# The scaling of attention probabilities by the reciprocal of their sums, issued on GpSimd instead of VectorE

## The chip, the core and the metric

The kernel runs on one core of a Trainium2 chip, as one program. The metric is the time of one execution on the device in microseconds (us), here as a median of runs. The core has four engines that compute: TensorE (PE, with its weight loads as PEld), VectorE (DVE), ScalarE (ACT) and GpSimd (POOL). SyncE (SP) issues most of the DMAs. Each engine works through its own list of instructions in order, and waits at an instruction until the semaphores that it names are set.

## What is computed

A layer with a state-space scan, a sparse attention and a mixture of 32 experts is followed by two layers with attention and a convolutional feed-forward part, one of them for two token streams. There are 256 tokens of 1024 features in each stream, in float32. The change concerns the softmax of four attentions. In the reference this is, for the grouped-query attention of the second part:

```python
def attend(q, k, v):
    s = jnp.einsum('bqhgd,bkhd->bhgqk', q, k) * scale
    p = softmax_f32(s).astype(v.dtype)
    return jnp.einsum('bhgqk,bkhd->bqhgd', p, v)

out_x = sweep_query_blocks(lambda qb: attend(qb, k_all, v_all), qx)...
out_c = attend(qc, kc, vc)... if ctx_out else None
```

The four are the selected and window branches of the first block (16 heads, 256 causal keys), the attention of the context stream in layer 0 (16 heads, 256 keys), that of the main stream in layer 0 (16 heads, 512 keys) and the latent attention of the main stream in layer 1 (16 heads, 512 keys).

## The kernel before

**Products of weights.** All weights are float32 and are split for TensorE into a high part and the rest. `split_weight` loads a piece `raw` by SyncE's queue, ScalarE rounds it to `whi` (L198), VectorE subtracts to get `wlo` (L199), and TensorE multiplies three times (L217 to L219). This runs through the whole program and is most of TensorE's and VectorE's work.

**Attention.** `nsa_attend` (first block) and `attend` (the three others) go by steps of two heads and one half or all of the 256 queries. A step has three parts. `scores` multiplies queries by keys into PSUM, takes the maxima on VectorE (L948 or L1465), makes the scaled negative of them (L951 or L1467) and lets ScalarE take the exponential, which also adds up the sums (L955 or L1471). `weigh` takes the reciprocal of the sums on VectorE (L959, L960 or L1477) and multiplies each row of probabilities by it, in place, one instruction for each head and half of queries (L964 or L1480). `turn` transposes the probabilities on TensorE (L973 or L1490) and copies them to SBUF, one head by VectorE and one by ScalarE; `combine` multiplies them by the values (L986 or L1498). The loop issues the scores of step n, `weigh` of step n-1 and `turn` of step n-2, so that the parts of three steps are under way at a time.

In layer 0 the scores are made from split queries and keys, three products for each head (L1710). The first head lies on one half of the array's rows and the second on the other.

**The order.** The attention generators are woven between other work: `weave` takes a unit of the side chains whenever their share of TensorE time is due. What `weave` gives is a sequence of calls only. A scheduler of the framework then orders the instructions of each engine by priorities and by its own estimates of when they can run, so a change of one instruction's engine shifts the order on all of them. Tiles come from rings of buffers by tag: `k2` for probabilities, `lin` and `aux` for PSUM banks.

**GpSimd before.** It does 12 additions of 128x256 beside the first block's attention (L761), powers for the norms (L507, L1551, L1746), and two DMA issues of constants.

Of the kernel before, what the change touches and what calls it, by code (L numbers as in the profile page):

```python
# [13 lines left out]
OP = mybir.AluOpType  # L14
# [65 lines left out]
# The quads of ada columns that are made beside the router and beside layer 0's attention.  # L80
Q2, Q3 = (0,), (1, 2)
# The rings that hold weights loaded ahead for the experts, before and after the phase's buffers are free.
ROOM = ("raw", "k4"), ("raw", "k4", "Q", "raw", "k4")
# How much of a side chain goes beside each step of the main one.
# [4 lines left out]
# The experts by their rank in number of tokens: the order of the units (rank of group, half) and their blocks.  # L89
# [3 lines left out]
# The 8 KB buffers: those of the second part lie where what the first part keeps there is done early.  # L93
# [5 lines left out]
class Kernel:  # L99
# [21 lines left out]
    @contextmanager  # L121
    def banks(self, **bufs):
        """The eight PSUM banks, cut into rings for one part of the program."""
        with self.tc.tile_pool(name="psum", bufs=1, space=bass.MemoryType.PSUM, reuse_waits="tile") as self.psum:
            self.psum_bufs = bufs
            yield

    @contextmanager
    def phase(self, **bufs):
        """Buffers that live for one part of the program."""  # L130
# [6 lines left out]
    def weave(main, *fills):  # L137
        """main with units of each (generator, share) among its own, by their TensorE time. A fill that yields None
        waits for main."""
# [30 lines left out]
    def passing(self, name, tag):  # L170
        """A constant that is needed only once."""
        which, a, n = self.cst_at[name]
        t = self.sb(tag, [P, n], name=name)
        self.A.dma_start(t, self.cst_ap[which][:, a:a + n])
        return t
# [6 lines left out]
    # ---------------------------------------------------------------- weights  # L182
# [5 lines left out]
    def split_weight(self, view):  # L188
        """(hi, lo) of each block of 128 rows of a view [128, n, cols]."""
# [14 lines left out]
    def flush(self):  # L204
        """Evictions are traced after the next weights' split, which TensorE waits for."""
# [15 lines left out]
    def lin_fm(self, W, c0, ncols, act, evict, k0=0, nk=None, more=False):  # L221
        """out^T: features on partitions. W [K, N] in DRAM; act (hi, lo) [128, nk, 256]."""
# [24 lines left out]
    def lin_tm(self, W, c0, ncols, act, evict, chunk=512):  # L247
        """out: tokens on partitions."""
# [25 lines left out]
    # ---------------------------------------------------------------- set-up  # L274
# [73 lines left out]
    def load_fm(self, src, h, tag, eng):  # L348
        """[256, 1024] rows of DRAM -> feature-major h [128, 8, 256]."""
# [16 lines left out]
    # ---------------------------------------------------------------- adaLN  # L366
# [11 lines left out]
    def take_bias(self, stg, dst):  # L378
        """The bias into dst [128, slots, 48], to which the products are added."""
# [5 lines left out]
    def ada_quad(self, W, q, dst, rsel):  # L385
        """Columns 2048q..2048q+2047 of silu(c) @ W onto dst [128, slots, 48]."""
# [17 lines left out]
    def ada_start(self, p):  # L404
        """Shift and scale of the first norm for half of the features, in the order of ada1."""
# [20 lines left out]
    def first_act(self, rb):  # L426
        """The first norm and the first two chunks of the token-major projection, by halves of the features as the
        modulation comes in."""
# [47 lines left out]
    # ---------------------------------------------------------------- norms  # L476
    def square_sums(self, h, nt, st, gain=None):
        """Sums of squares over features (32 times them) into the two columns of st: the column tiles of TensorE add up
        a quarter each."""
# [17 lines left out]
    def rms_bcast(self, h, nt, dim):  # L497
        """1/rms over features, one column per token, on all partitions (PSUM [128, 256])."""
# [11 lines left out]
    def spread(self, r, n):  # L510
        """Columns of r, one value per token, along the free dimension of all partitions."""
# [11 lines left out]
    def modulation(self, gain, ada, slot, vs, vsc):  # L523
        """gain * (1 + scale) and shift, [128, 8] each."""
# [15 lines left out]
    # ---------------------------------------------------------------- first block: projections  # L540
# [26 lines left out]
    def rope(self, x, nh, t, outs):  # L567
        """x [128, nh, 64] token-major, half-split rotation; written to each of outs."""
# [12 lines left out]
    def project_tm(self, act, pss):  # L581
        """dt, q, k/v, gates of the first block, tokens on partitions; the first two chunks are in pss."""
# [8 lines left out]
    def conv_silu(self, dst, ps, wname, bname, m, nm, taps):  # L591
        """Causal depthwise convolution over tokens, then silu."""
# [20 lines left out]
    # ---------------------------------------------------------------- SSD  # L613
# [40 lines left out]
    def ssd(self):  # L654
        """The chunked scan; y (with the skip) replaces the x channels. Yields where TensorE would wait."""
# [90 lines left out]
    def ssd_gate(self, act, sums):  # L746
        """y * silu(z), and its squares summed by group into sums [2][128, 2, 256]."""
# [35 lines left out]
    # ---------------------------------------------------------------- NSA  # L783
# [141 lines left out]
    def nsa_attend(self):  # L925
        """Selected and window branches (causal both: every block is chosen and the window spans the sequence)."""
# [30 lines left out]
        def weigh(i, t):  # L957
# [3 lines left out]
            for a in range(2):  # L961
                for b in range(2):
                    e = probs[i, t, a][:, b, :]
                    V.tensor_scalar(e, e, r[:, a, b:b + 1], None, OP.mult)  # L964
# [41 lines left out]
    # ---------------------------------------------------------------- first block  # L1006
    def sigmoid(self, out, x):
        """By tanh, whose table is the exponential's too."""
# [3 lines left out]
    def tanh_gates(self, act, c0, sg):  # L1012
        """tanh(x / 2): the sigmoid is half of one more."""
# [78 lines left out]
    # ---------------------------------------------------------------- mixture of experts  # L1092
    def router(self, h):
# [35 lines left out]
        def top(x):  # L1129
            """softmax over the 8 columns; its sorted values and their places."""  # L1130
# [847 lines left out]
```

## Time and profile before

| | us |
|---|---|
| median of 3 runs | 1766.12 |
| lowest and highest run | 1764.79, 1771.28 |
| the profiled execution, span from the first to the last instruction | 1765.9 |
| TensorE busy | 1690.6 |
| TensorE weight loads busy | 1379.4 |
| VectorE busy | 1272.3 |
| ScalarE busy | 917.8 |
| GpSimd busy | 42.4 |

The profile gives no other time for its own execution than the span. Busy time is the union of the instructions on an engine. TensorE's instructions overlap, and their ends are modelled, so a busy TensorE is not one at its peak. The granted clock is the share of full speed that TensorE had: 1.0 is 2.4 GHz and 0.5 is 1.2 GHz. A wait is put down to the semaphore that came last.

### The profile page before, as it was taken

Reading aid. Unit: us, or ns where it says so; the run is one execution under the profiler, and the core shown is the slowest. Engines: PE = TensorE matmul, PEld = TensorE weight load, DVE = VectorE, ACT = ScalarE, POOL = GpSimd, SP = SyncE. Lnnn points to the kernel's source line nnn. Section 1 sums busy time; section 2 is a strip of 40 time slices with the busy share of each in tenths; the row PEclk is TensorE's granted clock in tenths of the full one; section 3 lists DMA queues with packets and bytes.
Section 4 is the critical chain, followed back from the end, with each engine's and each line's share of the span. In section 5 each row is a group of like instructions: output and inputs, shape, how many; then the busy total and the mean of one; then the engine's idle time right before and its main releaser. Section 6 shows DMA issues by size and latency. Waiting matters only on the chain. (4 is left out here: it accounts for less than half of the span.)

```text
span 1765.9 us, 36466 instructions
## 1 busy us (share of the span) xinstructions
PE 1690.6 (96%) x12980; PEld 1379.4 (78%) x12980; DVE 1272.3 (72%) x3070; ACT 917.8 (52%) x1901; POOL 42.4 (2%) x48
## 2 busy tenths in 40 slices
PE   7999999999999999999999898999999989999998
PEld 3898777767876578888887554688999866789997
DVE  3997687675667768757756466968777788777876
ACT  2666446863443544534434252656665566556654
POOL 0000000100001000000000001000000000000000
PEclk8999999999999999999999988999999999999999
DMA  9756956849966997998999886234566432246662
GB/s 321 212 150 195 322 175 191 253 133 306 317 201 207 323 318 240 329 328 268 325 347 346 258 299 229 90 122 138 178 183 183 141 120 72 59 141 183 180 186 72
DMA packets 344962, 381.54 MB, mean 216 GB/s; under 512 B 27353, under 2 KB 298454, under 8 KB 344774
## 3 DMA queue, kind: packets, MB, share of 16 engines
q1 hardware_dynamic: 339456, 376.47, 67.2%
q10 hardware_dynamic: 5174, 1.97, 0.4%
q8 instruction: 104, 1.70, 0.4%
q0 software_dynamic: 144, 0.71, 0.1%
q14 instruction: 84, 0.69, 0.1%
HBM read 378.00 MB, written 1.05 MB: 215 GB/s over the span
## 5 line engine op out<-in xcount | busy, mean ns | idle before, releaser
L198 ACT CAST whi<-raw 128x512 fp32r<-128x512 f32 (+2 forms) x752 | 453.9, 610 | 383.9 <-PE lin L219 219.5
L199 DVE TENSOR_TENSOR wlo<-raw,whi 128x512 fp32r<-128x512 f32 (+2 forms) x752 | 502.4, 678 | 161.5 <-ACT whi L198 148.6
L217 PE MATMUL lin<-XA,whi 128*128 128x256 f32 x768 | 220.1, 287 | 1.7 <-ACT XA L465 1.7
L219 PE MATMUL lin<-XA,whi 128*128 128x256 f32 x768 | 219.0, 286 | 0.0
L218 PE MATMUL lin<-XA,wlo 128*128 128x256 f32 x768 | 218.9, 285 | 0.0
L217 PE MATMUL lin<-A,whi 128*128 128x256 f32 x576 | 168.4, 292 | 2.7 <-DVE k L598 1.9
L218 PE MATMUL lin<-A,wlo 128*128 128x256 f32 x576 | 163.5, 284 | 0.0
L217 PEld LDWEIGHTS lin<-XA,whi 128*128 128x128 f32 x768 | 149.3, 194 | 2.6 <-ACT XA L465 2.5
L218 PEld LDWEIGHTS lin<-XA,wlo 128*128 128x128 f32 x768 | 149.2, 194 | 0.7 <-issue 0.4
L219 PEld LDWEIGHTS lin<-XA,whi 128*128 128x128 f32 x768 | 148.9, 194 | 0.3
L217 PEld LDWEIGHTS lin<-A,whi 128*128 128x128 f32 x576 | 109.9, 191 | 33.8 <-issue 14.1
L219 PE MATMUL lin<-A,whi 128*128 128x256 f32 x448 | 127.7, 285 | 0.0
L217 PE MATMUL lin<-CA,whi 128*128 128x256 f32 x416 | 122.0, 293 | 0.3 <-ACT whi L198 0.2
L218 PE MATMUL lin<-CA,wlo 128*128 128x256 f32 x416 | 118.2, 284 | 1.1 <-DVE wlo L199 1.1
L219 PE MATMUL lin<-CA,whi 128*128 128x256 f32 x416 | 117.9, 283 | 0.0
L218 PEld LDWEIGHTS lin<-A,wlo 128*128 128x128 f32 x576 | 110.1, 191 | 0.9 <-issue 0.7
L1621 ACT ACTIVATE cv<-lin,vecs 128x256 f32<-128x256 f32 x132 | 73.9, 560 | 63.0 <-PE lin L219 52.7
L219 PE MATMUL lin<-XB,whi 128*128 128x256 f32 x352 | 99.4, 286 | 0.1
L1622 DVE SCALAR_TENSOR_TENSOR cv<-lin,vecs,cv 128x255 f32<-128x255 f32 x132 | 63.3, 480 | 49.4 <-ACT cv L1621 49.1
L217 PE MATMUL lin<-XB,whi 128*128 128x256 f32 x352 | 98.7, 283 | 0.0
L218 PE MATMUL lin<-XB,wlo 128*128 128x256 f32 x352 | 98.4, 283 | 0.0
L217 PEld LDWEIGHTS lin<-CA,whi 128*128 128x128 f32 x416 | 79.2, 190 | 15.5 <-issue 6.5
(534 smaller groups left out, 3835.0 us busy)
## 6 DMA issues: line engine op xcount, KB each, us to landing
raw<-in_ffn_w_up_dram SPq DMA_DIRECT2D x264, 256.0 KB
raw<-in_ada_w_dram SPq DMA_DIRECT2D x192, 256.0 KB
raw<-in_ffn_w_down_dram SPq DMA_DIRECT2D x132, 256.0 KB
raw<-in_w_in_dram SPq DMA_DIRECT2D x112, 256.0 KB
wx<-in_w_exp_gate_dram SPq DMA_DIRECT2D x112, 256.0 KB
wx<-in_w_exp_up_dram SPq DMA_DIRECT2D x112, 256.0 KB
wx<-in_w_exp_down_dram SPq DMA_DIRECT2D x112, 256.0 KB
raw<-in_w_ada_dram SPq DMA_DIRECT2D x96, 256.0 KB
```

Of the source, the lines that this page charges most:

```text
L198: self.A.copy(hi, raw)
L199: self.V.tensor_tensor(lo, raw, hi.bitcast(F32), OP.subtract)
L217: mm(out, whi, ahi, start=first, stop=False, skip_group_check=True)
L218: mm(out, wlo, ahi, start=False, stop=False, skip_group_check=True)
L219: mm(out, whi, alo, start=False, stop=last, skip_group_check=True)
L1621: A.activation(acc, ps, AF.Identity, bias=self.v(f"fb{i}", m), scale=self.v(f"fw{i}1", m))
L1622: V.scalar_tensor_tensor(acc[:, 1:], ps[:, 0:TOK - 1], self.v(f"fw{i}0", m), acc[:, 1:], OP.mult, OP.add)
```

## The change

In `weigh`, in both functions, the multiplication is issued on `self.G` (GpSimd) instead of `V` (VectorE). Operands, shapes and counts are the same: 64 instructions in `nsa_attend` (32 of 128x128 and 32 of 128x256) and 96 in `attend` (32 of 128x256 and 64 of 128x512). The other lines of the difference are comments.

```diff
@@ nsa_attend, weigh @@
             for a in range(2):
                 for b in range(2):
                     e = probs[i, t, a][:, b, :]
-                    V.tensor_scalar(e, e, r[:, a, b:b + 1], None, OP.mult)
+                    self.G.tensor_scalar(e, e, r[:, a, b:b + 1], None, OP.mult)
@@ attend, weigh @@
             V.reciprocal(sm, sm)
             for a in range(2):
                 for t in range(nt):
-                    V.tensor_scalar(pr[a][:, t, :], pr[a][:, t, :], sm[:, a, t:t + 1], None, OP.mult)
+                    self.G.tensor_scalar(pr[a][:, t, :], pr[a][:, t, :], sm[:, a, t:t + 1], None, OP.mult)
```

The scheduler's new order differs in many places, mostly in the four attentions. Three are shown, as a difference (- before, + after). The first is on GpSimd at the start of layer 0's attention; `s_14950` and `s_15121` are the powers for the norms of two pieces of the queries, `prob` the probabilities of the first steps by number.

```order
 L1551 TENSOR_TENSOR s_14950<-s_14949,mhalf_63 128x8 x2
+L1480 TENSOR_SCALAR prob_15107<-prob_15107,s_15102 128x512
+L1480 TENSOR_SCALAR prob_15108<-prob_15108,s_15102 128x512
 L1551 TENSOR_TENSOR s_15121<-s_15120,mhalf_63 128x8 x2
+L1480 TENSOR_SCALAR prob_15146<-prob_15146,s_15141 128x512
+L1480 TENSOR_SCALAR prob_15147<-prob_15147,s_15141 128x512
```

The powers stand behind the first step's two products, and the next step's products behind the powers.

The second is on TensorE in the middle of layer 0's attention. `lin_15495` and `lin_15496` are the two heads' scores of one step, each made by three products (L1710); `prob_15362` and `prob_15363` are the probabilities that are transposed.

```order
-L1710 MATMUL lin_15495<-khi_14578,qTx_14569 128x512
-L1710 MATMUL lin_15495<-khi_14578,qTx_14570 128x512
-L1710 MATMUL lin_15495<-klo_14571,qTx_14569 128x512
 L1490 MATMUL aux_15460<-ident_58,prob_15362 128x128 x4
 L1490 MATMUL aux_15466<-ident_58,prob_15363 128x128 x4
+L1710 MATMUL lin_15495<-khi_14578,qTx_14569 128x512
 L1710 MATMUL lin_15496<-khi_14578,qTx_14569 128x512
+L1710 MATMUL lin_15495<-khi_14578,qTx_14570 128x512
 L1710 MATMUL lin_15496<-khi_14578,qTx_14570 128x512
-L1710 MATMUL lin_15496<-klo_14571,qTx_14569 128x512
+L1710 MATMUL lin_15495<-klo_14571,qTx_14569 128x512
 L1498 MATMUL acc_15484<-pT_15425,vc_6566 64x256
```

The first head's scores move behind the transposes and stand between the second head's; the second head's last product moves behind the products with the values (L1498).

The third is on TensorE near the end of the first block's attention: the transposes (L973) of the last step but one, and the projection (`lin_4897`) that follows.

```order
 L973 MATMUL aux_4865<-ident_58,prob_4782 128x128 x2
 L973 MATMUL aux_4869<-ident_58,prob_4782 128x128 x2
+L219 MATMUL lin_4897<-D1_3056,whi_4900 128x256
+L217 MATMUL lin_4897<-D0_3055,whi_4906 128x256
 L218 MATMUL lin_4897<-D0_3055,wlo_4907 128x256
 L219 MATMUL lin_4897<-D1_3056,whi_4906 128x256
```

Products of the projection that stood ahead of these transposes stand behind them, so the transposes come earlier in the list.

## Rows read from the trace of the kernel before

**Rows 1.** Head of the page: the span, and each engine's busy us, share, instructions.

```profile
span 1765.9 us, 36466 instructions
...
PE 1690.6 (96%) x12980; PEld 1379.4 (78%) x12980; DVE 1272.3 (72%) x3070; ACT 917.8 (52%) x1901; POOL 42.4 (2%) x48
```

**Rows 2.** Busy time by stretch, us (columns: stretch, length, engines, granted clock, DMA share, GB/s).

```profile
240.00:385.00 145.00, 143.48 (x1038) 102.35 (x1037) 108.87 (x362) 98.49 (x247) 10.32 (x13) 1.00 0.59 185
575.00:630.00 55.00, 52.97 (x435) 28.96 (x436) 39.39 (x111) 28.49 (x88) 0.00 (x0) 1.00 0.96 307
1080.00:1105.00 25.00, 21.43 (x95) 7.38 (x96) 17.18 (x45) 6.71 (x14) 3.23 (x2) 0.80 0.67 224
1105.00:1152.00 47.00, 46.59 (x316) 29.77 (x313) 43.67 (x113) 32.45 (x84) 0.00 (x0) 1.00 0.23 75
1440.00:1530.00 90.00, 87.43 (x483) 58.96 (x482) 73.43 (x207) 56.53 (x133) 0.00 (x0) 1.00 0.19 61
```

**Rows 3.** Waits, 240 to 385 us, then 575 to 630 (waiter <- awaited: us, times, longest).

```profile
PE aux L973 <- DVE prob L964: 0.9, 1, 0.9
...
ACT prob L1471 <- DVE s L1467: 11.6, 5, 5.6
```

**Rows 4.** VectorE's groups by shape (count, busy us, mean ns, idle before).

```profile
L199 DVE TENSOR_TENSOR wlo<-raw,whi 128x512 fp32r<-128x512 f32 x684 | 464.9, 689 | 150.7 <-ACT whi L198 138.6 <-DMA wx<-in_w_exp_up_dram 1.9 <-PE lin L218 1.8
...
L1480 DVE TENSOR_SCALAR prob<-prob,s 128x512 f32<-128x512 f32 x64 | 28.5, 479 | 0.3
...
L1480 DVE TENSOR_SCALAR prob<-prob,s 128x256 f32<-128x256 f32 x32 | 9.8, 346 | 0.1
...
L964 DVE TENSOR_SCALAR prob<-prob,s 128x128 f32<-128x128 f32 x32 | 7.4, 280 | 0.1
```

**Rows 5.** GpSimd's groups by shape: its addition in the first block.

```profile
L761 POOL TENSOR_TENSOR sums<-sums,k 128x256 f32<-128x256 f32 x12 | 9.9, 824 | 332.8 <-ACT k L760 332.8
```

**Rows 6.** Timeline of GpSimd at 282 us; of all engines at 303 (start us, length us).

```profile
282.51 0.94 POOL L761 TENSOR_TENSOR sums<-sums,k 128x256 f32<-128x256 f32 x1 [262.46 <-ACT k L760]
...
303.05 0.73 POOL L761 TENSOR_TENSOR sums<-sums,k 128x256 f32<-128x256 f32 x1 [2.27 <-ACT k L760]
...
303.31 1.01 DVE L199 TENSOR_TENSOR wlo<-raw,whi 128x512 fp32r<-128x512 f32 x1
```

**Rows 7.** Timeline of TensorE in layer 0's attention.

```profile
1111.56 0.73 PE L1710 MATMUL lin<-khi,qTx 64*128 64x512 f32 x4
...
1112.48 0.72 PE L1710 MATMUL lin<-khi,qTx 64*128 64x512 f32 x2
...
1113.37 1.09 PE L1490 MATMUL aux<-ident,prob 128*128 128x128 f32 x8
...
1117.16 1.09 PE L1490 MATMUL aux<-ident,prob 128*128 128x128 f32 x8
1118.18 0.50 PE L1710 MATMUL lin<-khi,qTx 64*128 64x512 f32 x2
```

**Rows 8.** Timeline of VectorE in the same stretch.

```profile
1114.06 0.15 DVE L1477 RECIPROCAL s<-s 128x2 f32<-128x2 f32 x1
...
1114.78 0.87 DVE L1480 TENSOR_SCALAR prob<-prob,s 128x512 f32<-128x512 f32 x2
```

**Rows 9.** Timeline of all engines at the first block's last steps.

```profile
371.94 0.15 DVE L960 TENSOR_TENSOR s<-s,gate 128x4 f32<-128x4 f32 x1
...
373.25 0.63 PE L973 MATMUL aux<-ident,prob 128*128 128x128 f32 x4 [0.88 <-DVE prob L964]
...
378.45 0.16 DVE L960 TENSOR_TENSOR s<-s,gate 128x4 f32<-128x4 f32 x1
...
379.58 1.09 PE L973 MATMUL aux<-ident,prob 128*128 128x128 f32 x8
```

**Rows 10.** Timeline of all engines at layer 1's second step.

```profile
1456.15 0.15 DVE L1477 RECIPROCAL s<-s 128x2 f32<-128x2 f32 x1
...
1457.72 0.71 PE L1490 MATMUL aux<-ident,prob 128*128 128x128 f32 x5
```

## The prediction

> **What bounds the kernel now.** I read the head of the page first. The span is 1765.9 us and TensorE is busy for 1690.6 us of it, 96%; VectorE 1272.3 us, GpSimd 42.4 us [rows 1]. The reader is to see that VectorE, which the change relieves, has over 490 us of spare time, and that TensorE has 75. Then the busy time by stretch, for the four stretches in which attention runs: the first block's (240 to 385 us), the context's beside the experts (575 to 630), layer 0's (1105 to 1152) and layer 1's (1440 to 1530) [rows 2]. TensorE is idle there for 1.52, 2.03, 0.41 and 2.57 us, 6.5 us together. That is all a faster VectorE could give back inside them, unless TensorE's own order gets better. In the second stretch the DMA engines are 96% busy as well, with the experts' weights, so idle time there need not come back at all.
>
> Third, the waits of TensorE. In the first stretch one wait of 0.9 us is for a product of the probabilities [rows 3], and it is the only one that the view puts down to them there. So the multiplication hardly ever ends a wait of the engine that sets the end.
>
> **What goes.** VectorE loses 160 instructions. The 128x512 form takes 479 ns (64 of them), the 128x256 form 346 ns in the later attention (32), the 128x128 form 280 ns (32) [rows 4]; the first block's 32 of 128x256 I take at the same 346. That is 30.7 + 11.1 + 11.1 + 9.0 = 62 us of VectorE's busy time, beside TensorE's work nearly all of it. What I give it on TensorE's path: the 0.9 us wait and a part of the idle time that VectorE's queue causes elsewhere, 1.5 us of the 6.5.
>
> **What comes.** GpSimd gets the same 160 products, and no trace row shows one there. Bounds of a 128x512 product: from below VectorE's own 0.479 us [rows 4]. From above the nearest row on GpSimd, an addition of two 128x256 tensors at 0.824 us on average and 0.73 us where nothing is in its way [rows 5, 6]; twice the size makes 1.46 us, and it reads two tensors where the product reads one and a scalar. I take the middle, 1.0 us, and 0.55 us for 128x256 (between 0.346 and 0.73), 0.4 us for 128x128. The Trainium skill (GPSIMD Engine Reference, section 3.1, Elementwise) gives 769 ns as measured for a tight loop over 512 elements; no run here shows it, and by that price the terms for late products below would shrink to about 0.5 us.
>
> What matters is not GpSimd's sum (about 64 + 35 + 13 = 112 us, in four stretches of 337 us) but how late each product is. In layer 0, VectorE's reciprocal starts at 1114.06, its two products start only at 1114.78, because a copy and a small product stand in front, and TensorE turns the result at 1117.16 [rows 7, 8]. So 2.95 us lie between the end of the reciprocal (1114.21) and the transposes, and GpSimd, which has nothing in front, ends its two by 1114.21 + 0.05 + 2.0 = 1116.3. Two products of 1.0 us per step also fit into a step of 3.3 us (two steps run from 1111.56 to 1118.18, where the 1117.16 transposes take their 1.02 us). I made the same subtraction for the other steps. In layer 0 and layer 1, 28 of the 32 steps have 1.8 us or more to the first transpose. The step at 1456.15 has 1.42 us (end of reciprocal 1456.30, transposes 1457.72) [rows 10], which is enough for the first product and 0.2 us short for the second. The step just ahead of 1105 is some 0.4 us short. In the first block the first ten steps have 14 us and more. Its last ones are tight: products are asked for at 372.09 and wanted at 373.25, asked for at 378.61 and wanted at 379.58 [rows 9]. There two products of 0.55 us come 0.1 to 0.2 us late, the second pair 0.3 us and 0.85 us. I take 1.3 us for the first block, 0.4 for layer 0, 0.2 for layer 1, nothing for the context (its tightest step has 2.35 us for two products of 0.55).
>
> **What the new order does.** The scheduler places everything anew. In layer 0 the six score products of a step are two chains on different halves of the array: interleaved they take 0.92 us (1111.56 to 1112.48), one chain alone takes 0.89 us (1112.48 to 1113.37), so two of them 1.78 [rows 7]. Before, every second step is split in two; after, three of these steps are interleaved up to the last product, which saves 1.78 - 1.2 = 0.6 us each (two interleaved pairs and two single products: 0.34 + 0.23 + 2 x 0.32), and an earlier one too, but two steps near the end become split, for 0.7 us each. Sum: -1.8 - 0.8 + 1.4 = -1.2 us. GpSimd's powers for the norms of the queries (L1551) now stand behind two products in its queue; the products end by about 1086.1 and the power started at 1086.26, so this costs nothing, and up to 1 us if a product takes 1.46.
>
> **What the two engines do to each other.** The trace shows it. While GpSimd's addition ran from 303.05 for 0.73 us, VectorE's subtraction from two SBUF tensors (L199) that started at 303.31 took 1.01 us instead of the group's 0.69 [rows 4] and ended 0.54 us after it. The other way round, an addition started at 282.51 under a VectorE operation took 0.94 [rows 6]. So each product can hold a VectorE operation of that kind for 0.3 us and be held by one as long. 160 products at 0.3 us are 48 us on VectorE at the worst, less than the 62 us it is spared, and TensorE meets only what exceeds its slack. None of TensorE's waits in these stretches is for L199's output, so little of it reaches the path: I take 1.0 us, with 0 and 10 us (a fifth of the 48) as bounds.
>
> **Sum.** 1765.9 - 1.5 + 1.3 + 0.4 + 0.2 - 1.2 + 1.0 = 1766.1 us. The median of the runs, 1766.12, is 0.2 us above the profiled span, which I let stand. I predict 1766 us, with 1761 to 1772 as this case's own range.
>
> **Rivals.**
> 1. GpSimd becomes the late engine (slower). If a 128x512 product takes the upper bound, 1.46 us, and is held 0.3 us by VectorE, two of them make 3.5 us, more than layer 0's step of 3.3: 14 steps x 0.2 = 3 us there. The tight steps then lose about 7 us (1.5 us before 1105, 0.7 at layer 0's end, 2.5 in layer 1, 2.6 in the first block), and a few us of VectorE's delays reach TensorE: 1766 + 3 + 7 + 3 = 1779 us. It decides from 1.65 us per product with its waits on. For it: the collision rows, and that GpSimd's addition is slow for its size. Against: the product has one tensor input, and most steps have 2 us of slack. The Trainium skill (SBUF — State Buffer, Who interferes with whom) has the shared port pair held for a whole instruction by whichever engine starts first; the 303.31 row agrees. Four products in a row in the first block would by that rule hold VectorE longest.
> 2. VectorE's queue is the hidden bound (faster). In the context stretch ScalarE waited 11.6 us for the small product on VectorE that stands in front of the exponential [rows 3], and in layer 0 VectorE is 43.67 us busy of 47 [rows 2]. If all 6.5 us of idle time goes, the new order brings its 1.2, and the 3.6 us in which TensorE is idle from 1080 to 1105 [rows 2] go too: 1765.9 - 11.3 = 1754.6 us. Against: TensorE is busy for 46.59 of layer 0's 47 us, and the wait at 1080 is in front of the first exponential, where no product is late.
> 3. The new order alone moves the time, by when TensorE idles. From 1080 to 1105 the granted clock averaged 0.80 [rows 2], so the half level, 1.2 GHz, stood there for about 0.4 of 25 us, 10 us, after TensorE had sat idle. One such stretch more or less is 5 us at full speed: 1761 or 1771 us.
>
> **Chances.** The forecast 0.56, the first rival 0.19, the second 0.15, the third 0.10. A measurement of this kernel can tell about 0.5%, 8.8 us, from no change. The forecast and the third rival lie within it; of the first rival nearly all is beyond it, of the second most, with a little of the others past either end. That makes faster 0.15, same 0.65, slower 0.20. The range takes in the second rival's near half and the first rival up to its price: 1756 to 1779.
>
> **What would show it.** Right: GpSimd's line on the page at 110 to 160 us and VectorE's near 1215 to 1240; the 128x512 product on GpSimd between 0.8 and 1.2 us; TensorE's idle time in the four stretches within 4 us of the 6.5; two steps of layer 0 in 6.0 to 6.7 us. L199's mean grows by some tens of ns in the first block. Wrong: TensorE waiting for L964 or L1480 on GpSimd step after step, a layer 0 step longer than 3.4 us, or the clock falling in a stretch where it is 1.00 now.

## The result: 13.6 us slower

The changed kernel takes 1780.47 us (median of 4 runs, 1780.28 to 1785.73) where the kernel before takes 1766.86 (4 runs beside it, 1764.79 to 1771.28). The ratio is 1.0077, with a 95% interval of 1.0057 to 1.0097. The forecast was 1766 us with a range up to 1779, so the time lies just past the upper end, and past the 0.5% that was to separate slower from no change. It is the outcome of the first rival, GpSimd as the late engine, and at nearly its price of 1779 us.

The profiled execution spans 1778.6 us (1780.37 with what lies around it), 12.7 us more than that of before. Head of the page of the changed kernel (answers [rows 1]):

```profile
span 1778.6 us, 36677 instructions
...
PE 1690.5 (95%) x12980; PEld 1377.4 (77%) x12980; DVE 1235.5 (69%) x2910; ACT 918.4 (52%) x1901; POOL 226.9 (13%) x208
```

TensorE is busy as long as before in the sum over the whole span, so the 12.7 us show as idle time there; by stretch its busy time moves too, as the rows below show. VectorE lost 37 us where I had summed 62: the durations that I summed overlap (together they fill 55.4 us before), and some of VectorE's other instructions grew. GpSimd gained 184 where I had summed 112, and its groups by shape (count, busy us, mean ns, idle before and what ended it) say why; the last row answers [rows 5]:

```profile
L1480 POOL TENSOR_SCALAR prob<-prob,s 128x512 f32<-128x512 f32 x64 | 100.4, 1586 | 79.8 <-DVE s L1477 56.0 <-PE aux L1490 17.1 <-PE lin L1848 4.2
L964 POOL TENSOR_SCALAR prob<-prob,s 128x256 f32<-128x256 f32 x32 | 33.3, 1058 | 31.7 <-DVE s L960 27.0 <-PE lin L218 3.1 <-ACT prob L955 1.6
L1480 POOL TENSOR_SCALAR prob<-prob,s 128x256 f32<-128x256 f32 x32 | 29.7, 946 | 26.8 <-DVE s L1477 21.9 <-DVE hots L1263 3.4 <-PE S L1687 1.6
L964 POOL TENSOR_SCALAR prob<-prob,s 128x128 f32<-128x128 f32 x32 | 22.5, 718 | 252.9 <-DVE s L960 241.0 <-ACT whi L198 11.9
...
L761 POOL TENSOR_TENSOR sums<-sums,k 128x256 f32<-128x256 f32 x12 | 9.0, 748 | 13.7 <-ACT k L760 13.6
```

Undisturbed, a product takes 1.56, 0.92 and 0.60 us for 512, 256 and 128 columns (medians 1563, 923 and 603 ns). I had taken 1.0, 0.55 and 0.4, with 1.46 and 0.73 as upper ends for the first two. Both are above their upper end, and the third is half as dear again as I took it: the product, which reads one tensor, is slower on GpSimd than the addition of two tensors of the same size in the last row.

Busy time by stretch after (columns as in [rows 2]: PE, PEld, DVE, ACT, POOL, granted clock, DMA share, GB/s):

```profile
240.00:385.00 145.00, 139.69 (x1006) 99.76 (x1004) 94.85 (x299) 97.66 (x246) 65.18 (x77) 1.00 0.57 179
575.00:630.00 55.00, 53.03 (x427) 29.38 (x425) 30.47 (x72) 26.50 (x80) 27.90 (x30) 1.00 0.85 268
1105.00:1152.00 47.00, 42.46 (x265) 23.87 (x264) 34.47 (x77) 26.70 (x66) 34.00 (x22) 1.00 0.41 137
...
349.30:417.00 67.70, 61.64 (x406) 0.97 0.50 160
...
1109.20:1172.00 62.80, 57.49 (x402) 1.00 0.25 83
```

Compared with [rows 2], TensorE's idle time grew from 1.5 to 5.3 us in the first stretch and from 0.4 to 4.5 in layer 0. The last two rows (TensorE's busy time only) are cut at the same TensorE instructions as these two of the kernel before, the end of the first block and layer 0:

```profile
350.00:410.00 60.00, 57.55 (x402) 1.00 0.52 167
...
1100.80:1160.00 59.20, 58.23 (x401) 1.00 0.28 92
```

The first block's end takes 67.7 us instead of 60, layer 0's attention 62.8 instead of 59.2. Of the first block's 7.7 us, 4.1 are longer busy time of TensorE; layer 0's 3.6 are all idle time. What TensorE waits for there, after (355 to 400 us, then 1095 to 1170):

```profile
PE aux L973 <- POOL prob L964: 3.9, 8, 0.6
...
PE aux L1490 <- POOL prob L1480: 4.7, 5, 1.5
```

And the steps themselves. The timelines of the engines, after, in the first block's step that answers [rows 9]:

```profile
372.47 0.16 DVE L960 TENSOR_TENSOR s<-s,gate 128x4 f32<-128x4 f32 x1
...
372.82 5.94 POOL L964 TENSOR_SCALAR prob<-prob,s 128x256 f32<-128x256 f32 x8 [1.59 <-ACT prob L955]
...
373.80 0.44 PE L973 MATMUL aux<-ident,prob 128*128 128x128 f32 x2 [0.64 <-POOL prob L964]
374.70 0.44 PE L973 MATMUL aux<-ident,prob 128*128 128x128 f32 x2 [0.46 <-POOL prob L964]
...
376.50 0.44 PE L973 MATMUL aux<-ident,prob 128*128 128x128 f32 x2 [0.46 <-POOL prob L964]
```

TensorE transposes two 128x128 pieces as each product ends, then mostly waits 0.46 us for the next: its transposes come at GpSimd's beat of 0.90 us. The eight products (two steps, merged by the view) are one unbroken row of 5.94 us. The same in layer 0, from the step that the prediction has just ahead of 1105 (its transposes, at 1114.25 here, started at 1105.79 before):

```profile
1112.62 9.27 POOL L1480 TENSOR_SCALAR prob<-prob,s 128x512 f32<-128x512 f32 x6 [14.08 <-DVE s L1477]
...
1113.87 0.15 DVE L1477 RECIPROCAL s<-s 128x2 f32<-128x2 f32 x1
1114.25 0.66 PE L1490 MATMUL aux<-ident,prob 128*128 128x128 f32 x4 [1.45 <-POOL prob L1480]
1115.79 0.65 PE L1490 MATMUL aux<-ident,prob 128*128 128x128 f32 x4 [0.46 <-POOL prob L1480]
```

Three steps' products stand back to back. The reciprocal that ends at 1114.02 finds GpSimd busy until 1115.73 with the step before.

The next step is that of [rows 7, 8]:

```profile
1123.94 0.15 DVE L1477 RECIPROCAL s<-s 128x2 f32<-128x2 f32 x1
...
1124.28 6.18 POOL L1480 TENSOR_SCALAR prob<-prob,s 128x512 f32<-128x512 f32 x4 [2.38 <-ACT pT L1492]
...
1124.39 0.39 PE L1710 MATMUL lin<-klo,qTx 64*128 64x512 f32 x1
1125.90 0.44 PE L1490 MATMUL aux<-ident,prob 128*128 128x128 f32 x2 [1.12 <-POOL prob L1480]
```

GpSimd is free and starts 0.19 us behind the end of the reciprocal, and the product still comes 1.12 us late. TensorE is done with its scores at 1124.78, only 0.69 us behind the reciprocal. Before, the transposes of this step came 2.95 us behind it: the scheduler's new order leaves less work of TensorE in between.

### The profile page after: what moved, and what is told of

It is laid out like the page before. It is cut to its first block, busy times and chain, and to the rows that moved or that the text cites. A ratio compares the mean times of both kernels' runs of the same rounds, so it can differ in the third digit from the quotient of the medians.

```text
span 1778.6 us, 36677 instructions
## 1 busy us (share of the span) xinstructions
PE 1690.5 (95%) x12980; PEld 1377.4 (77%) x12980; DVE 1235.5 (69%) x2910; ACT 918.4 (52%) x1901; POOL 226.9 (13%) x208
## 5 line engine op out<-in xcount | busy, mean ns | idle before, releaser
L199 DVE TENSOR_TENSOR wlo<-raw,whi 128x512 fp32r<-128x512 f32 (+2 forms) x752 | 504.1, 680 | 175.9 <-ACT whi L198 163.0
L1480 POOL TENSOR_SCALAR prob<-prob,s 128x512 f32<-128x512 f32 (+1 forms) x96 | 130.1, 1372 | 106.6 <-DVE s L1477 77.9
```

What stands on the lines that cost most here:

```text
L199: self.V.tensor_tensor(lo, raw, hi.bitcast(F32), OP.subtract)
L1480: self.G.tensor_scalar(pr[a][:, t, :], pr[a][:, t, :], sm[:, a, t:t + 1], None, OP.mult)
```

## The experiments

Three theories: **A**, the product is dear on GpSimd and comes late; **B**, the two engines hold each other up at SBUF, where their tiles lie; **C**, the scheduler's new order and the clock, not the products. All ratios are to the kernel before, run beside each, with 95% intervals; in us of 1767:

| run | ratio | interval | us |
|---|---|---|---|
| whole change | 1.0077 | 1.0057 to 1.0097 | +13.6 |
| e1 first block only | 1.0041 | 1.0025 to 1.0057 | +7.2 |
| e2 later three only | 1.0045 | 1.0030 to 1.0061 | +8.0 |
| e3 shadow products | 0.9994 | 0.9982 to 1.0006 | -1.1 |
| e5 later three, half products | 1.0009 | 0.9998 to 1.0020 | +1.6 |
| e6 second head only | 1.0033 | 1.0021 to 1.0045 | +5.8 |
| e7 first ten steps only | 0.9999 | 0.9988 to 1.0010 | -0.2 |
| e8 context only | 1.0017 | 1.0007 to 1.0026 | +3.0 |
| e10 two-tensor form | 1.0032 | 1.0018 to 1.0045 | +5.7 |
| e11 layers 0 and 1 only | 1.0028 | 1.0016 to 1.0040 | +4.9 |
| e12 only where there is room | 1.0005 | 0.9991 to 1.0019 | +0.9 |

e4's time answers no theory (below), and e9 was run once (1766.99 us), for its trace.

Where it arises, from one trace each: the n-th TensorE instruction of a line and operand is set against the n-th in the kernel before, and the median difference of their starts is taken at ten cuts (us in the time of before). An entry is what a stage adds to the lag.

| run | to 230 | to 345 | first block's end, to 410 | to 545 | context, to 645 | experts, to 960 | to 1090 | layer 0, to 1160 | to 1435 | layer 1, to 1545 | rest |
|---|---|---|---|---|---|---|---|---|---|---|---|
| whole | 0.6 | -1.3 | 7.7 | 0.0 | 2.2 | 1.8 | -2.6 | 3.6 | -0.7 | 1.6 | -0.3 |
| e1 | -0.4 | -1.4 | 8.3 | 0.3 | 0.2 | 1.2 | -1.5 | -0.1 | -1.3 | 1.3 | -1.1 |
| e2 | -0.2 | 0.0 | 0.7 | 0.1 | 3.1 | 1.0 | -2.2 | 3.4 | 0.2 | 1.7 | -1.1 |
| e3 | 1.3 | 0.1 | 0.1 | 0.4 | 0.9 | 2.4 | -0.6 | 0.1 | -0.4 | 0.1 | 0.0 |
| e5 | 1.2 | 0.0 | 0.4 | 0.1 | 2.2 | 1.5 | -1.0 | -0.5 | 0.2 | 0.0 | -0.2 |
| e6 | 1.0 | 1.0 | 1.4 | 0.2 | 2.0 | 0.4 | -1.8 | -0.6 | 0.3 | -0.8 | 0.0 |
| e7 | 2.0 | -1.2 | 0.2 | 0.1 | 0.0 | 1.6 | -4.2 | 0.2 | -0.4 | 0.4 | -0.1 |
| e8 | 1.3 | -0.1 | 0.0 | 0.1 | 2.4 | 2.5 | -0.7 | 1.2 | 0.3 | 1.0 | -1.2 |
| e10 | 2.1 | -1.0 | 3.3 | 0.4 | 2.0 | 1.8 | -4.4 | -0.3 | -2.2 | 1.2 | -0.2 |
| e11 | -0.3 | 0.0 | 0.0 | 0.0 | 0.0 | 0.2 | -2.6 | 3.0 | -0.4 | 1.7 | -0.4 |
| e12 | 0.7 | -1.0 | 0.7 | 0.1 | 1.6 | 0.5 | 0.1 | 0.3 | -0.1 | 1.6 | 0.1 |

Columns without attention (start, experts, ahead of layer 0) move by 2 us and more whatever the edit, so that is the grain of a single trace. The first block's end and layer 0 stand far above it. The cut at 1090 lies where the granted clock changes (0.50 from 1082.8 to 1093.1 before), and shifts up to 1.5 us between its two neighbours (e10, e12). Cut at TensorE's instructions from the transposes at 1101.33 to the end of layer 0 instead, that stretch takes 58.9 us before, 62.3 to 62.6 in the three runs with whole products there (whole, e2, e11) and 58.0 to 59.6 in all the others.

**e1, first block only, and e2, later three only.** The one line of L1480, or of L964, goes back to VectorE:

```
-  self.G.tensor_scalar(pr[a][:, t, :], pr[a][:, t, :], sm[:, a, t:t + 1], None, OP.mult)
+  V.tensor_scalar(pr[a][:, t, :], pr[a][:, t, :], sm[:, a, t:t + 1], None, OP.mult)
```

> Only the first block's 64 products (L964) are issued on GpSimd; the later three attentions keep theirs on VectorE. In the trace of the changed kernel TensorE's work of the first block's last steps (356 to 408 us) ends some 7.7 us later against the kernel before, and the rest of the loss lies in the later attentions. Theory A (late products: a product costs GpSimd 0.92 us for 128x256 and 0.60 for 128x128, three times what VectorE needs, and TensorE waits for it where a step has less room): 7 us slower than before, 5 to 9, with TensorE waiting for L964's output 3 to 5 us between 355 and 400. Theory B (the two engines hold each other up at SBUF): about as much, so that this run alone doesn't tell A from B. Theory C (the scheduler's new order of the instructions and the clock stretches that come with it, not the products): the first block's order hardly differs, so within 2 us of before.

> Only the later three attentions' 96 products (L1480) are issued on GpSimd; the first block keeps its on VectorE. Theory A: what the first block cost is gone and what the later stretches cost stays, 6 us slower than before, 3 to 8 (context stretch 2, experts 2, layer 0 4, layer 1 1.5, less 2 to 3 that the clock gave back ahead of layer 0); with the run of the first block alone it adds up to the whole change's 13 us. Theory C: all of the 13 us here, since here the order of TensorE's instructions differs most.

Measured +7.2 and +8.0 us, 15.2 together against 13.6, so the parts add up. C expected all of it in e2 and none in e1: C alone falls.

**e3, shadow.** VectorE keeps its products in all four attentions, and on the same line of the first block GpSimd does one more, on a scratch tile:

```
+  self.G.tensor_scalar(shadow[:, 0:P * (t + 1)], shadow[:, 0:P * (t + 1)], r[:, a, b:b + 1], None, OP.mult)
```

> VectorE keeps all its products as in the kernel before. In the first block GpSimd does as many further products of the same sizes, from the same reciprocals at the same time, on a scratch tile that nobody reads, so that only the two engines' effect on each other is left. Theory A: nobody waits for these, so within 2 us of before (1765 to 1769). Theory B (collisions): most of the first block's loss comes without the late products, 5 to 8 us slower than before, and VectorE's two-input operations in 240 to 400 us lengthened by over 10 us in all.

Measured -1.1 us, interval through zero, and 0.1 us at the first block's end. The shadows ran, and both engines felt them (e3's groups from 240 to 400 us, GpSimd then VectorE):

```profile
L964 POOL TENSOR_SCALAR shadow<-shadow,s 128x256 f32<-128x256 f32 x32 | 34.4, 1076 | 28.3 <-DVE s L960 25.4 <-ACT prob L955 0.6
...
L964 DVE TENSOR_SCALAR prob<-prob,s 128x256 f32<-128x256 f32 x32 | 12.7, 454 | 0.1
```

VectorE's product took 454 ns on average; before it was 364 in the same stretch. Collisions are real: the VectorE operations that ran beside GpSimd's took 6.8 us more in all than by the medians of before. None of it reached TensorE. B falls for the first block. For layer 0 no shadow was run, but two traces answer it. GpSimd's products are not held there (1563 ns on average from 1109 to 1172 us, as undisturbed). VectorE's small product in front of the exponential (L1467) is, as its rows for layer 0's attention show, before, after and in e10 (below):

```profile
L1467 DVE TENSOR_SCALAR s<-s 128x2 f32<-128x2 f32 x14 | 2.2, 157 | 0.0
L1467 DVE TENSOR_SCALAR s<-s 128x2 f32<-128x2 f32 x14 | 4.5, 322 | 0.0
L1467 DVE TENSOR_SCALAR s<-s 128x2 f32<-128x2 f32 x14 | 5.0, 360 | 0.0
```

In e10 it is held longest, and e10 loses nothing in layer 0. So B isn't layer 0's loss either.

**e4, half products everywhere.** `pr[a][:, t, 0:n // 2]` and likewise in the first block.

> The changed kernel, with each product done only for the first half of its columns on GpSimd (the other half of the probabilities stays unscaled). TensorE's order is that of the changed kernel but for two places. A product should then take 0.95, 0.60 and 0.45 us for the three sizes, close to what the prediction took for whole ones (1.0, 0.55, 0.4). Theory A: the late products all but go, within 3 us of before (1764 to 1770), and TensorE's wait for L964 and L1480 falls to under 3 us in all. Theory B: half of the loss stays, 6 us slower than before. Theory C: the order is as in the changed kernel, so the whole loss stays, 11 to 14 us slower than before.

Measured 1913.66 us (ratio 1.0834), which answers no theory. With the first block's result changed, the tokens choose other experts and the rest of the program works longer. I should have seen that the router stands behind this attention. Only its trace up to the experts can be read: the first block's end lags 4.5 us, not 7.7, with products of 0.60 and 0.44 us. That is less, but more than A left for the whole kernel (3).

**e5, half products in the later three.** As e2, with `0:n // 2`.

> As the run of the later three attentions, but each of their products is done only for the first half of its columns on GpSimd (the other half stays unscaled; the first block is whole, on VectorE). The order on VectorE, ScalarE and SP's queue is exactly that of the later three, TensorE's but for a few rows; only the price of a product falls, to about 0.95 us for the 128x512 and 0.6 us for the 128x256 probabilities. Theory A (late products): layer 0's 3.5 us and layer 1's loss go, TensorE waits less than 1 us for L1480 from 1080 to 1165 (3.2 us with whole products). Theory C (order): nothing goes, 7.5 us slower than before. I hold A for layers 0 and 1, and C for the context's stretch, where TensorE waits for no product and the weights' loads stand in another order in SP's queue: there 2 to 3 us of lag stay, so 3 to 4 us slower than before in all.

Measured +1.6 us instead of e2's 8.0, with the same order of instructions on nearly all engines. In layer 0 the 3.4 us are gone, and of TensorE's wait, 3.2 us in e2, this is left (1090 to 1165 us):

```profile
PE aux L1490 <- POOL prob L1480: 1.0, 2, 0.5
```

So layer 0's loss hangs on the product's duration. The context's 2.2 us stay, as expected, but I had put the total at 3 to 4.

**e6, second head only.** `(self.G if a else V).tensor_scalar(...)` in both places.

> In all attentions VectorE multiplies the first head of each pair, which TensorE turns first, and GpSimd the second, which it turns half a microsecond later. Theory A: a product of 1.56 us that starts right behind the reciprocal ends inside the second head's room in nearly every step (least 1.46 us in the first block, where two of 0.92 us are wanted, and 1.66 us in layer 0), so nearly all of the late products' loss goes: first block +1 us instead of +8, layers 0 and 1 +1 instead of +4. With 2 to 3 us in the context's stretch for the order of SP's loads: 1 to 4 us slower than before, and 9 us faster than the changed kernel. Theory C: as much order is changed as in the changed kernel, 10 us slower than before or more.

Measured +5.8 us where 1 to 4 was expected. Its trace shows what A expected in the first block (1.4 instead of 7.7) and layer 0 (-0.6), but that execution was the fastest of its six (1770.72). The interval runs from 3.7 to 8.0 us, and the medians differ by 4.2, so the miss may be a small one. What the other executions lose on top is not in the trace and stays open.

**e7, first ten steps only.** `(self.G if i < 5 else V)` in the first block, the rest on VectorE.

> Only the first block's first ten steps (40 of its 64 products, which have 14 us and more to the transposes) are issued on GpSimd; its last six steps, whose room is 1.0 to 5 us, and the later attentions stay on VectorE. Theory A: nothing is late, so the 8 us of the first block's end (356 to 410 us) are gone, no half-clock stretch stands at 384, and the 1.4 us stay that the stretch around 250 us gave back: 1.5 us faster to 1 us slower than before. A rival (GpSimd's products cost the first block something wherever they stand, since VectorE's wider order changes): 3 us slower than before or more.

Measured -0.2 us. Forty products of e1's 64 cost nothing; the 24 of the last six steps cost the 7 us. The length of the first block's end in e7, cut as above:

```profile
350.85:411.03 60.18, 57.49 (x401) 1.00 0.52 164
```

**e8, context only, and e11, layers 0 and 1 only.** `(self.G if nkt == 2 else V)`, and `nkt == 4`.

> Only the context attention's 32 products (beside the experts) are issued on GpSimd. SP's queue is then exactly as in the run of the later three: FFN weights stand ahead of experts' weights. If the context's loss comes from that order: TensorE's work lags 2 to 3 us behind the kernel before at 600 to 650 us, waits for wx from DMA, and some of it is given back ahead of layer 0, so 1 to 4 us slower in all, layers 0 and 1 with no further loss. If it comes from late products in the context (GpSimd's 0.92 us each, four a step): the same lag here, but none in the run with half products. If neither: within 1 us of before.

> Only layer 0's and layer 1's products (64 of 128x512) are issued on GpSimd; SP's queue is as in the kernel before. If the context's loss is its own and the parts add up: no lag at 600 to 650 us, 3 to 4 us of lag from 1090 to 1160, about 1 in layer 1, 4.6 us slower than before in all (3 to 6), which with the context's 3.0 makes the 7.6 us of the later three.

Measured +3.0 and +4.9, 7.9 together against e2's 8.0. In e11 the context's stretch is as before (0.0) and layer 0 lags 3.0. In the context the six traces with its products on GpSimd, whole or half or dealt between the engines, lag 2.0 to 3.1 us, and no matmul of TensorE waits for one of them. What it waits for in e8 and not before (570 to 600 us) is one copy on VectorE and one load of weights:

```profile
PE aux L1490 <- DVE pT L1492: 0.9, 1, 0.9
PE acc L1317 <- DMA wx<-in_w_exp_gate_dram: 0.8, 1, 0.8
```

These are not the price: e11 waits 0.6 us for such a load too and doesn't lag. The scheduler had split pairs of score products that ran interleaved before, and these products (L1687) show the loss themselves (565 to 660 us; before, e8, e11):

```profile
L1687 PE MATMUL S<-kT,qTc 64*128 64x256 f32 x64 | 13.7, 412 | 1.2 <-ACT prob L1471 0.7 <-ACT qTc L1591 0.4
L1687 PE MATMUL S<-kT,qTc 64*128 64x256 f32 x64 | 15.7, 415 | 0.6 <-ACT qTc L1591 0.4
L1687 PE MATMUL S<-kT,qTc 64*128 64x256 f32 x64 | 13.7, 412 | 0.5 <-ACT qTc L1591 0.4
```

The same 64 products keep TensorE busy for 15.6 to 15.7 us in all six, and for 13.7 before and in the runs that leave the context alone (e1, e3, e7, e11). That price of the order is C's share: TensorE's own work, not a wait. The queue of loads isn't it: by the names of the tensors SP issues in e2, e5 and e8 in the order of before until some 690 us, and the lag has come by 627. e12, whose context products are those of before, lags 1.6 us there for another reason: its granted clock was 0.50 from 582.36 to 585.77, and the lag comes in that one step.

**e9, the price by itself.** On a scratch tile in the first block, four forms in turn (written out here, in the edit one function):

```
+  G.tensor_scalar(o, o, k, None, OP.mult)      G.tensor_scalar(o, o, 0.5, None, OP.mult)
+  G.tensor_tensor(o, o, k.to_broadcast([P, o.shape[1]]), OP.mult)      G.tensor_copy(o, cmp_rep)
```

> The price by itself. VectorE does all products as before; in the first block GpSimd does 64 operations on a scratch tile that nobody reads, in four forms in turn (heads pairs 0 and 4, 1 and 5, 2 and 6, 3 and 7): product by a scalar per partition, product by a constant, product with the reciprocal spread as a second tensor, plain copy; on 128x128 and 128x256. If a product with a scalar per partition is what is dear: 0.60 and 0.92 us for it, 0.45 and 0.73 us for the two-tensor form (the addition's size), and the constant and the copy at or under these. If GpSimd is as slow with any form: all four within 0.1 us of 0.60 and 0.92.

GpSimd's groups in e9 (means, with VectorE's interference):

```profile
L928 POOL TENSOR_SCALAR shadow<-shadow,s 128x256 f32<-128x256 f32 x8 | 9.4, 1173 | 11.5 <-DVE s L960 10.9
L928 POOL TENSOR_SCALAR shadow<-shadow 128x256 f32<-128x256 f32 x8 | 7.9, 989 | 0.6
...
L928 POOL TENSOR_TENSOR shadow<-shadow,s 128x256 f32<-128x256 f32 x8 | 5.2, 652 | 2.0 <-DVE s L960 1.5
L928 POOL COPY shadow<-cst 128x256 f32<-128x256 f32 x8 | 4.8, 599 | 0.4
```

The shortest of each are 922, 847, 612 and 400 ns. A tensor by a scalar is the dearest form; that the scalar is one per partition adds only 75 ns. The constant was not cheap, against what I expected. The product of two tensors, one of them the reciprocal spread along the row, does the same arithmetic in two thirds of the time.

**e10, the two-tensor form in the real kernel.** The change with

```
+  self.G.tensor_tensor(pr[a][:, t, :], pr[a][:, t, :], sm[:, a, t:t + 1].to_broadcast([P, n]), OP.mult)
```

and the same in the first block; every engine's order is that of the changed kernel.

> The changed kernel with each product written as a product of two tensors (the reciprocal spread along the row) instead of a tensor and a scalar per partition; the order of the instructions is the same on every engine. If that form costs what GpSimd's addition costs (0.73 us for 128x256, about 1.2 to 1.4 us for 128x512), theory A makes the loss fall between that with half products and that with whole ones: 6 to 10 us slower than before instead of 13.6. If the form costs the same or more: 13 us or more. Theory C: 13 us whatever the form costs.

GpSimd's groups in e10:

```profile
L1480 POOL TENSOR_TENSOR prob<-prob,s 128x512 f32<-128x512 f32 x64 | 66.7, 1064 | 106.8 <-DVE s L1477 71.9 <-PE aux L1490 22.4 <-PE lin L1848 5.8
L964 POOL TENSOR_TENSOR prob<-prob,s 128x256 f32<-128x256 f32 x32 | 22.8, 743 | 35.7 <-DVE s L960 33.9 <-ACT prob L955 1.8
L1480 POOL TENSOR_TENSOR prob<-prob,s 128x256 f32<-128x256 f32 x32 | 18.6, 612 | 35.8 <-DVE s L1477 32.8 <-PE S L1687 3.1
L964 POOL TENSOR_TENSOR prob<-prob,s 128x128 f32<-128x128 f32 x32 | 14.8, 491 | 256.1 <-DVE s L960 243.6 <-ACT whi L198 11.9 <-PE aux L973 0.6
```

Measured +5.7 us, cheaper than I expected, since the form costs 1.04, 0.61 and 0.40 us undisturbed. With nothing changed but the product's form and so its duration, about 8 of the 13.6 us go (some 4 to 12 with both intervals). That is the strongest case for A. It also is a rerun of my forecast at the prices that I had assumed, 1.0, 0.55 and 0.4, and it still is 5.7 us slower: the price is not all that went wrong.

**e12, only where there is room.** Two-tensor products in the first ten steps and for the second head of layers 0 and 1, all others on VectorE.

> A version put together from the runs so far: products in the two-tensor form on GpSimd only where the room is enough (the first block's first ten steps; the second head of each pair in layers 0 and 1), all others on VectorE, the context's too. By theory A nothing is late and by the order theory the context's stretch is as before: from 3 us faster (1.3 us given back in the first block, as in the run of the first ten steps, and part of TensorE's idle time in layer 1) to 1 us slower than before. If it still is 3 us slower or more, something that neither names goes with every product on GpSimd. No measurable gain is expected, since VectorE's products ended one wait of 0.9 us only.

Measured +0.9 us, interval 0.9991 to 1.0019: no gain to be measured, which a relief of VectorE could not bring while TensorE is the bound. No version tried beats the kernel before by more than its interval.

## Why the prediction was wrong, step by step

**Right: what bounds the kernel and where it would hurt.** TensorE is the bound, VectorE's relief brought nothing, and the tight steps named in [rows 9] and in layer 0 are the places that lost most. e7 shows that the ten steps with 14 us of room lost nothing, as said. The 1.5 us that I gave to VectorE's relief did not show: e7 measured -0.2 and e12 +0.9, both with intervals through zero.

**Wrong: the price of a product (1.0, 0.55 and 0.4 us).** This is the step that failed. The upper bound was built on "it reads two tensors where the product reads one and a scalar", so the addition of [rows 5] was to be dearer. It is the other way round: 923 ns for the product of 128x256, 738 for the addition (medians). The reason was not in a row; it was an analogy from operand counts. The bound therefore did not hold, and the middle that I took was the price of a form that the change does not use. The runs put this error at some 8 us (13.6 against e10's 5.7); the two terms that follow, and the context, are the rest. The Trainium skill's GPSIMD Engine Reference (section 4.1, Engine selection) says the same as I did, that one-input operations on GpSimd are "roughly line-rate" and two-input ones slower; for this form the measurement decides against it. The Trainium skill's 769 ns for 512 elements (same page, section 3.1, Elementwise), by which the late terms were to shrink, stands against 1563 ns here.

**Wrong: the first block's term (+1.3 us).** At the assumed price (e10) its end still lags 3.3 us, and 7.7 in the changed kernel. My 1.3 us were waits for late products alone, and at the assumed price these are near it, 1.1 us (e10's transposes, 351 to 414.4 us):

```profile
L973 PE MATMUL aux<-ident,prob 128*128 128x128 f32 x48 | 8.4, 288 | 1.5 <-POOL prob L964 1.1
```

What I left out is that four products in a row set the beat of all eight transposes, which then run in pairs and are busy longer themselves (8.4 us here, 7.3 before). Of the changed kernel's 7.7 us, TensorE's groups (columns: count, busy us, mean ns, idle before) show these parts; before, then after, same cuts as above:

```profile
L973 PE MATMUL aux<-ident,prob 128*128 128x128 f32 x48 | 7.3, 281 | 0.9 <-DVE prob L964 0.9
...
L986 PE MATMUL acc<-pT,vt 128*64 128x256 f32 (+1 forms) x64 | 6.7, 333 | 0.1
```

```profile
L973 PE MATMUL aux<-ident,prob 128*128 128x128 f32 x48 | 8.8, 293 | 4.0 <-POOL prob L964 3.9
...
L986 PE MATMUL acc<-pT,vt 128*64 128x256 f32 (+1 forms) x64 | 8.0, 369 | 0.7 <-DVE pT L974 0.7
```

Waits for products grew by 3.1 us. The 48 transposes are busy 1.5 us longer, since pairs that stand alone don't overlap as a row of eight does (0.44 us for a pair above, 1.09 us for eight in [rows 9]). L986 takes 1.3 us longer, for the most part by the clock (in e10, which has no such stretch, 0.5): the granted clock was 0.50 from 384.35 to 387.76, the 1.2 GHz level, after TensorE had waited in every product of the last step. That is what I listed as a sign of being wrong, though it is not the products' doing alone: e2 and e5, with VectorE's products there, have such a stretch at 385 too, and it cost them 0.4 to 0.7 us. The scheduler also moved four of L391's products there (46 instead of 42), while 1.3 us were given back between 245 and 290 us.

**Wrong: layer 0's terms (+0.4 - 1.2 us).** They measured +3.6, all idle time: TensorE's busy time fell by 0.7 us (58.23 to 57.49), so the new order did bring part of its 1.2. Two products of 1.54 us back to back fill 3.1 us of a step of 3.3; one late step delays the next. With half the work (e5) the lag is -0.5 and in e10 -0.3 (-0.9 and +0.1 by the cut at the transposes), near the forecast's -0.8 for layer 0. So the size of one term, the product, was off. The room was off as well, which cheaper products nearly hide: I read 2.95 us in the order of before, and the new order left 0.69 us at that step (in e5 and e10 too).

**Partly wrong: the context at nothing.** No product is late there, as said. But the new order in the context costs 2 to 3 us (e8, +3.0), of which the split score products are 2.0. It is the effect that I had worked out for layer 0, and for layer 0 alone.

**Collisions (+1.0 us).** None that can be measured in the first block (e3), and none that layer 0's loss follows (e10). L199's mean in the first stretch even fell, from 717 to 702 ns (240 to 400 us), where some tens of ns more were foretold. The Trainium skill (SBUF — State Buffer, Who interferes with whom) has one engine block the other for a whole instruction; e3's 364 to 454 ns agree with its direction, and the slack took it in.

**Too small: layer 1 (+0.2).** It lags 1.6, and in the three runs with whole products there (whole, e2, e11) TensorE waits for them (after, 1452 to 1558 us):

```profile
PE aux L1490 <- POOL prob L1480: 1.6, 3, 0.9
```

The 1.3 and 1.6 of e1 and e12 are not products: in both the granted clock was 0.50 for 3.4 us at the start of this stretch, from 1445.3 and from 1442.5. e10 lags 1.2 with only 0.2 us of such waits; what the rest is stays open.

The first rival had the right engine. It gave a late product 1.76 us with its waits and 14 steps x 0.2 in layer 0; at 1.56 without collisions layer 0 lost 3.6 us. Not VectorE's delays made up the rest, as it had it, but the first block and the context's order.

## What to carry to other kernels

An operation that is moved to another engine is priced by a row of the same form, not by one with more operands; where there is none, the upper end of the range belongs well above the nearest row, and a scratch copy of the operation that nobody waits for measures it without disturbing the kernel. Where several moved operations run one behind the other, the consumer moves at their beat, so compare the whole row with the step, not the first one with its room. The room itself has to be read in the order that the change brings: here it shrank from 2.95 to 0.69 us at one step, and in the context the order alone cost 2 us. And an engine that isn't the bound has nothing to give: the relief of VectorE was worth 0 even where no product was late.

## What the runs showed of the hardware that was not expected

On GpSimd the form decides more than the number of operands. From 128 to 256 columns (the shortest of each in e9) the product by a scalar grows by 320 ns (602 to 922), by a constant 319, the two-tensor product with the spread reciprocal 214, a copy 110: 2.5, 2.5, 1.7 and 0.9 ns per column, on top of 0.18 to 0.28 us for each instruction. The same product costs 1563 ns for 512 columns as tensor by scalar and 1040 as tensor by tensor (medians), where VectorE needs 479 [rows 4].
